# Latent attention: the reciprocal row sums are spread behind the products with the values

## The chip, the cores and the metric

The kernel runs on one core of one Trainium2 chip. Its time is the device time of one execution in microseconds (us), as the median of several runs. Each number in the profile comes from one profiled execution.

## The reference

The reference runs two transformer blocks over 1024 positions of width 1024, in float32. The first has a state-space branch and a latent attention branch; the second has windowed attention and a gated feed-forward part. The change lies in the latent attention: four heads, 192 dimensions of queries and keys, 128 of values, causal:

```
s = einsum('bqhd,bkhd->bhqk', qb, k) * scale
s = where(causal, s, -inf)
pr = softmax(s, axis=-1)
out = einsum('bhqk,bkhd->bqhd', pr, v)
ym = out * silu(gm)                      # the gate, taken from another projection
```

## The kernel before

The attention stage is `block1b` (lines 718 to 869). It loops over four heads (`hd`) and, in each, over four groups of 256 queries (`g`): 16 groups. A group has two blocks of 128 queries. For each block TensorE forms the scores (`sp`, line 811), VectorE adds the mask and takes the maximum (`negmax`), ScalarE takes the exponential into `P` and adds up each row into `ls`, TensorE transposes `P` in pieces of 128x128 (`tp`, line 826), and ScalarE and VectorE split the transposed piece into a high and a low float32r half (`PT`).

The softmax is not divided by its sum before the product with the values. Instead the reciprocal of the sum (line 833) stands as one number for each query, on partitions. The output of the product is transposed (128 value dimensions on partitions, 256 queries along the row), so the reciprocal must lie along the row and be the same on all partitions. TensorE does that: it transposes the column, broadcast to 128x128, into PSUM (`lb`, lines 834 to 836). VectorE multiplies `lb` by 0.5 and by the loaded gate into `gl` (line 839). TensorE multiplies values and transposed exponentials into `po` (lines 840 to 844), three matmuls for each of `2g + 2` key blocks, so 6, 12, 18 or 24 of them. VectorE multiplies `po` by `gl` into `y` (line 846, tile `yo` in the profile), which is stored.

`lb` and `po` are tiles of the PSUM pool `mlaps` with the tag `mm`, which has two buffers. The same two buffers serve every projection tile `ps` of the stage: the queries and keys of the next head (`project`), the values (`values`, evacuated by `vl`), the gate of the state-space branch (`glu`, evacuated by `gst`), and the output products (`out_ys`, evacuated by `xst`). The scores have four buffers of their own, the transposed pieces two.

The order on each engine is not that of the text. A planner (`schedule_with_timeline_sim=True`) goes through the program with modelled durations and picks, for each engine, among the instructions whose inputs and buffers are there by its own clock; text that stands earlier goes first. The engines then work through these fixed orders, and semaphores hold back what comes too early. `self.after(a, b)` (line 140) adds an edge to this plan, without a semaphore: `b` stands behind `a`.

Of the kernel before, what the change touches and what calls it, by code (L numbers as in the profile page):

```python
# [10 lines left out]
F32 = mybir.dt.float32  # L11
F32R = mybir.dt.float32r
I32 = mybir.dt.int32
ALU = mybir.AluOpType
# [37 lines left out]
class Kernel:  # L52
# [665 lines left out]
    def block1b(self):  # L718
        nc, tc, I = self.nc, self.tc, self.I
# [4 lines left out]
        pp = self.open("mlaps", space=PSUM, bufs=2)  # L724
# [26 lines left out]
        def project(hd):  # L751
            qk = [[ma.tile([128, 1024], F32R, name=f"{n}{a}", tag=f"{n}{a}", bufs=2) for a in "hl"] for n in "qk"]

            def evac_q(mt, th, ps):
                hs = slice(th * 512, th * 512 + 512)
                self.split_ps(ps, qk[0][0][:, hs], qk[0][1][:, hs])

            def evac_k(mt, th, ps):
                hs = slice(th * 512, th * 512 + 512)
                self.split_ps(ps, qk[1][0][:, hs], qk[1][1][:, hs], scale)  # L760

            self.dense([[hd]], None, 2, CQ, evac_q, pp, pre={hd: [w[:, 256 * hd:] for w in wq]})
            self.dense([[hd]], None, 1, CK, evac_k, pp, pre={hd: [w[:, 128 * hd:] for w in wkv]})
            return qk + [rotated(hd)]

        def values(pair):
            wh, wl = (w[:, 512 + 256 * pair:] for w in wkv)
            for tk in range(4):
                ps = pp.tile([128, 2, 256], F32, name="ps", tag="mm", bufs=2)
                for j in range(2):  # L770
                    s = slice((2 * tk + j) * 128, (2 * tk + j) * 128 + 128)
                    for n, (a, b) in enumerate(((ck[0], wh), (ck[0], wl), (ck[1], wh))):
                        nc.tensor.matmul(ps[:, j], a[:, s], b[:, :256], start=n == 0, stop=n == 2)
                self.split_ps(ps, V[0][:, 2 * tk:2 * tk + 2], V[1][:, 2 * tk:2 * tk + 2])
# [8 lines left out]
        for hd in range(4):  # L783
            if hd == 2:
                values(1)
            for ch in ((0,), (1,), (2,), (3,))[hd]:
                self.ada_acc(ch, True)
            (qh, ql), (kh, kl), qs_ = qk
            vs = slice((hd % 2) * 128, (hd % 2) * 128 + 128)
            for g in range(4):  # L790
                PT = [m2.tile([128, 2 * g + 2, 256], F32R, name=f"pt{a}", tag=f"pt{a}{g % 2}", bufs=1) for a in "hl"]
                ls = m2.tile([128, 2, 2], F32, name="ls", tag="ls", bufs=3)
                if g < 2:
                    nc.gpsimd.memset(ls[:, :, 1], 0.0)
                for x in PT:
                    nc.gpsimd.memset(x[:, 2 * g + 1, 0:128].bitcast(F32), 0.0)
                for j in range(2):
                    qi = 2 * g + j
                    nk = 128 * (qi + 1)
                    nch, w = (1, max(nk, 256)) if nk <= 512 else (2, nk // 2)  # L800
                    we = min(w, nk)
                    qs = slice(qi * 128, qi * 128 + 128)
                    mx = m2.tile([128, 2], F32, name="mx", tag="mx", bufs=3)
                    P = m2.tile([128, 1024], F32, name="P", tag="P", bufs=2)
                    sps = []
                    for c in range(nch):
                        sp = pp.tile([128, 512], F32, name="sp", tag="S", bufs=4)
                        k = slice(c * w, c * w + w)
                        ops = ((qh, kh), (qh, kl), (ql, kh), (qs_, KS[0]), (qs_, KS[1]))
                        for n, (a, b) in enumerate(ops):  # L810
                            nc.tensor.matmul(sp[:, :w], a[:, qs], b[:, k], start=n == 0, stop=n == 4)
                        self.negmax(sp[:, :we], (ctab[:, 640 - we:] if c == nch - 1 else ctab)[:, :we], mx[:, c:c + 1])
                        sps.append(sp)
                    rq = self.rq[:, qi:qi + 1]
                    if nch == 1:
                        self.tt(mx[:, 0:1], mx[:, 0:1], rq, ALU.mult)
                    else:
                        self.stt(mx[:, 0:1], mx[:, 0:1], mx[:, 1:2], rq, ALU.min, ALU.mult)
                    for c in range(nch):
                        self.act(P[:, c * w:c * w + we], sps[c][:, :we], AF.Exp, bias=mx[:, 0:1],  # L820
                                 scale=self.nrq[:, qi:qi + 1], accum=ls[:, j, c:c + 1])
                    for k0 in range(0, qi + 1, 4):
                        n = min(4, qi + 1 - k0)
                        tp = pp.tile([128, 4, 128], F32, name="tp", tag="T", bufs=2)
                        for k in range(n):
                            nc.tensor.transpose(tp[:, k], P[:, (k0 + k) * 128:(k0 + k + 1) * 128], self.ident)
                        self.split_ps(tp[:, :n], PT[0][:, k0:k0 + n, j * 128:j * 128 + 128],
                                      PT[1][:, k0:k0 + n, j * 128:j * 128 + 128])
                ls2 = m2.tile([128, 2], F32, name="ls2", tag="ls2", bufs=3)
                self.tt(ls2, ls[:, :, 0], ls[:, :, 1], ALU.add)  # L830
                ls = ls2

                nc.vector.reciprocal(ls, ls)
                lb = pp.tile([128, 2, 128], F32, name="lb", tag="mm", bufs=2)
                for j in range(2):
                    nc.tensor.transpose(lb[:, j], ls[:, j:j + 1].to_broadcast([128, 128]), self.ident)
                gl = m2.tile([128, 256], F32, name="gl", tag="gl", bufs=2)
                nc.sync.dma_start(gl, self.g2_d[4 + hd][:, 256 * g:256 * g + 256])
                self.stt(gl, lb.rearrange("p a b -> p (a b)"), 0.5, gl, ALU.mult, ALU.mult)
                po = pp.tile([128, 256], F32, name="po", tag="mm", bufs=2)  # L840
                for k in range(2 * g + 2):
                    for n, (a, b) in enumerate(((V[0], PT[0]), (V[0], PT[1]), (V[1], PT[0]))):
                        nc.tensor.matmul(po, a[:, k, vs], b[:, k, :], start=k == 0 and n == 0,
                                         stop=k == 2 * g + 1 and n == 2)
                y = m2.tile([128, 256], F32, name="yo", tag="yo", bufs=2)
                self.tt(y, po, gl, ALU.mult)
                nc.sync.dma_start(self.ysm_d[4 + hd][:, 256 * g:256 * g + 256], y)
                if g == 1 and hd < 3:
                    qk = project(hd + 1)
                if (hd, g) == (2, 1):  # L850
                    self.wo = {mt: self.load_w(self.wo_src(mt), 1024) for mt in range(4)}
                if (hd, g) == (2, 3):

                    self.load_ys(1, self.cqp, "cq")
                for mt in YSF.get((hd, g), ()):
                    self.out_ys(mt, pp)
                for ch in {(2, 0): (0,), (3, 0): (1,), (3, 2): (2,)}.get((hd, g), ()):
                    self.ada_fin(ch, pp, "T", 2)
            if hd < 2:
                self.glu(hd, pp)  # L860
            if hd == 1:
                self.load_ys(0, ysp, "y0")
# [1291 lines left out]
```

## Time and profile before

| what | value |
|---|---|
| median of three runs | 2269.06 us (2267.28 to 2270.81) |
| the profiled execution | 2265.56 us |
| its span, first to last instruction | 2263.5 us |
| mean granted TensorE clock | 0.972 |
| TensorE matmul busy | 2122.7 us (94%), 10216 instructions |
| VectorE busy | 1502.9 us (66%) |
| ScalarE busy | 969.7 us (43%) |
| GpSimd busy | 1124.1 us (50%) |

In the profile PE is TensorE's matmul, PEld its weight load, DVE is VectorE, ACT ScalarE, POOL GpSimd, SP SyncE. L836 is line 836 of the kernel; lines 83, 86, 102 and 111 are those of helpers that many places call, so one goes by the tile's name there. A wait for several semaphores is put down to the one that came last. Idle time of an engine that is not the bottleneck costs nothing.

### The profile page before, as it was taken

Reading aid. Unit: us, or ns where it says so; the run is one execution under the profiler, and the core shown is the slowest. Engines: PE = TensorE matmul, PEld = TensorE weight load, DVE = VectorE, ACT = ScalarE, POOL = GpSimd, SP = SyncE. Lnnn points to the kernel's source line nnn. Section 1 sums busy time; section 2 is a strip of 40 time slices with the busy share of each in tenths; the row PEclk is TensorE's granted clock in tenths of the full one; section 3 lists DMA queues with packets and bytes.
Section 4 is the critical chain, followed back from the end, with each engine's and each line's share of the span. In section 5 each row is a group of like instructions: output and inputs, shape, how many; then the busy total and the mean of one; then the engine's idle time right before and its main releaser. Section 6 shows DMA issues by size and latency. Waiting matters only on the chain.

```text
span 2263.5 us, 29117 instructions
## 1 busy us (share of the span) xinstructions
PE 2122.7 (94%) x10216; PEld 1766.0 (78%) x10216; DVE 1502.9 (66%) x2511; ACT 969.7 (43%) x1717; POOL 1124.1 (50%) x728
## 2 busy tenths in 40 slices
PE   5998999899999989999999898999899999989998
PEld 4776777777877778888887786888688888877887
DVE  8969976652486345545656862435987777777676
ACT  4222345432245356666444442223544444455223
POOL 4625556665554545654423333523455555535471
PEclk8999999999999999999999899999999999999999
DMA  7433345555654555555345545442122222234332
GB/s 274 137 101 108 92 122 177 177 172 182 199 172 166 175 167 170 171 171 150 121 136 158 166 159 181 169 139 102 47 84 84 84 84 84 84 130 135 98 126 80
DMA packets 186973, 313.25 MB, mean 138 GB/s; under 512 B 43512, under 2 KB 85068, under 8 KB 186828
## 3 DMA queue, kind: packets, MB, share of 16 engines
q1 hardware_dynamic: 186828, 311.40, 43.0%
q8 instruction: 80, 1.31, 0.2%
q14 instruction: 65, 0.53, 0.1%
HBM read 225.65 MB, written 80.96 MB: 135 GB/s over the span
## 4 chain that ended last, share of the span: by engine, by line
PE 41%; DVE 6%; DMA 2%; issue 1%; ACT 1%; POOL 1%; SPq 0%; POOLq 0%; DVEq 0%; ACTq 0%
PE u L1704 17%; PE ps L137 4%; PE ps L135 4%; PE ps L136 4%; PE pd L1885 3%; PE pd L136 2%; PE pd L135 2%; PE pd L137 2%; PE po L1386 1%; DMA ox<-o_d 1%; DVE P L90 1%; PE tp L1378 1%; DVE x L86 1%; DMA as<-a_d 1%; DVE a L86 1%
## 5 line engine op out<-in xcount | busy, mean ns | idle before, releaser
L111 POOL TENSOR_TENSOR wl<-wst,wh 128x1024 fp32r<-128x1024 f32 (+2 forms) x159 | 398.3, 2507 | 488.8 <-ACT wh L102 454.4
L102 ACT ACTIVATE wh<-wst 128x1024 fp32r<-128x1024 f32 (+1 forms) x164 | 168.3, 1028 | 274.2 <-PE ps L136 115.2
L83 POOL TENSOR_TENSOR acc<-acc,wa 128x512 f32<-128x512 f32 x84 | 110.5, 1316 | 16.6 <-ACT wa L102 13.3
L135 PE MATMUL ps<-xh,wh 128*128 128x512 f32 x256 | 103.3, 404 | 4.2 <-DVE kb L83 2.7
L135 PE MATMUL ps<-h1h,wh 128*128 128x512 f32 x256 | 102.5, 400 | 2.8 <-DVE qz L86 2.1
L135 PE MATMUL ps<-h0h,wh 128*128 128x512 f32 x256 | 103.9, 406 | 0.6 <-ACT wh L102 0.6
L137 PE MATMUL ps<-h0h,wl 128*128 128x512 f32 x256 | 102.9, 402 | 0.7 <-POOL wl L111 0.6
L136 PE MATMUL ps<-h0l,wh 128*128 128x512 f32 x256 | 103.1, 403 | 0.0
L136 PE MATMUL ps<-h1l,wh 128*128 128x512 f32 x256 | 102.7, 401 | 0.0
L137 PE MATMUL ps<-xh,wl 128*128 128x512 f32 x256 | 102.0, 399 | 0.0
L136 PE MATMUL ps<-xl,wh 128*128 128x512 f32 x256 | 101.9, 398 | 0.0
L137 PE MATMUL ps<-h1h,wl 128*128 128x512 f32 x256 | 101.9, 398 | 0.0
L83 POOL TENSOR_TENSOR tb<-rt,grid 128x384 f32<-128x384 f32 x48 | 43.1, 906 | 117.0 <-DVE mx L886 88.9
L135 PE MATMUL pd<-Ah,wh 128*128 128x512 f32 (+1 forms) x256 | 93.8, 366 | 5.4 <-ACT s L102 5.4
L136 PE MATMUL pd<-Al,wh 128*128 128x512 f32 (+1 forms) x256 | 93.8, 366 | 0.5 <-DVE Al L111 0.5
L137 PE MATMUL pd<-Ah,wl 128*128 128x512 f32 (+1 forms) x256 | 92.8, 366 | 0.0
L83 DVE TENSOR_TENSOR z<-r,wst 128x512 f32<-128x512 f32 x40 | 71.6, 1790 | 24.5 <-POOL wl L111 24.0
L886 DVE CUSTOM_DVE_ANT_0 sp<-sp,tab 128x256 f32<-128x256 f32 (+1 forms) x128 | 52.7, 425 | 41.8 <-PE sp L163 26.4
L90 POOL TENSOR_SCALAR wa<-wa,sc 128x512 f32<-128x512 f32 x36 | 56.9, 1582 | 47.0 <-DMA wa<-in_w_ada 45.3
L111 POOL TENSOR_TENSOR wl<-z,wh 128x1024 fp32r<-128x1024 f32 (+1 forms) x28 | 63.9, 2282 | 30.8 <-ACT wh L102 27.2
L102 ACT ACTIVATE a<-a 128x1024 f32<-128x1024 f32 x22 | 23.4, 1063 | 108.9 <-DVE a L86 108.8
L83 DVE TENSOR_TENSOR s<-s,pd 128x512 f32<-128x512 f32 x76 | 51.0, 681 | 27.9 <-PE pd L137 14.1
(595 smaller groups left out, 7086.3 us busy)
## 6 DMA issues: line engine op xcount, KB each, us to landing
wa<-in_w_ada SPq DMA_DIRECT2D x96, 256.0 KB, 3.1
wst<-in_w_in SPq DMA_DIRECT2D x47, 512.0 KB, 4.0
wst<-in_w_up SPq DMA_DIRECT2D x24, 512.0 KB, 3.3
a_d<-a SPq DMA_DIRECT2D x22, 512.0 KB, 2.6
wst<-in_w_down SPq DMA_DIRECT2D x22, 512.0 KB, 3.6
as<-a_d SPq DMA_DIRECT2D x22, 512.0 KB, 3.6
r<-in_w_up SPq DMA_DIRECT2D x20, 512.0 KB, 3.2
wst<-in_w_out SPq DMA_DIRECT2D x16, 512.0 KB, 3.3
```

The costliest lines, as they stand in the source:

```text
L83: (eng or self.nc.vector).tensor_tensor(out, a, b, op)
L86: self.nc.vector.scalar_tensor_tensor(out, a, s, b, op0=op0, op1=op1)
L90: (eng or self.nc.vector).tensor_scalar(out, a, s1, None, op0=op0)
L102: self.nc.scalar.activation(out, a, f, **kw)
L111: self.last_lo = e.tensor_tensor(lo, y, hi.bitcast(F32), ALU.subtract)
L135: first = mm(ps, wh, xh, start=start, stop=False)
L136: mm(ps, wh, xl, start=False, stop=False)
L137: mm(ps, wl, xh, start=False, stop=stop)
L886: self.nc.vector.tensor_tensor_reduce(out=s, in0=s, in1=tab, scale=-1.0, scalar=-NEG, op0=ALU.add, op1=ALU.min, accum_out=m)
L1378: nc.tensor.transpose(tp[:, g], P[:, g], self.ident)
L1704: nc.tensor.matmul(ps, x[:, s], y[:, k], start=first and n == 0, stop=k == 3 and n == 2, skip_group_check=True)
L1885: nc.tensor.matmul(ps, w[u][:, 128 * k:128 * k + 128], x[v], start=start and k == i == 0, stop=k == 1 and i == 2, skip_group_check=True)
```

## The change

The transposes into `lb` and the product of `lb` with the gate are moved behind the matmuls into `po`. Both transposes get an edge behind the group's last matmul, so they follow it in TensorE's order. The tile `po` now takes its buffer ahead of `lb`. The load of the gate keeps its place in the text, behind the reciprocal.

```diff
                 nc.vector.reciprocal(ls, ls)
-                lb = pp.tile([128, 2, 128], F32, name="lb", tag="mm", bufs=2)
-                for j in range(2):
-                    nc.tensor.transpose(lb[:, j], ls[:, j:j + 1].to_broadcast([128, 128]), self.ident)
                 gl = m2.tile([128, 256], F32, name="gl", tag="gl", bufs=2)
                 nc.sync.dma_start(gl, self.g2_d[4 + hd][:, 256 * g:256 * g + 256])
-                self.stt(gl, lb.rearrange("p a b -> p (a b)"), 0.5, gl, ALU.mult, ALU.mult)
                 po = pp.tile([128, 256], F32, name="po", tag="mm", bufs=2)
                 for k in range(2 * g + 2):
                     for n, (a, b) in enumerate(((V[0], PT[0]), (V[0], PT[1]), (V[1], PT[0]))):
-                        nc.tensor.matmul(po, a[:, k, vs], b[:, k, :], start=k == 0 and n == 0,
-                                         stop=k == 2 * g + 1 and n == 2)
+                        last = nc.tensor.matmul(po, a[:, k, vs], b[:, k, :], start=k == 0 and n == 0,
+                                                stop=k == 2 * g + 1 and n == 2)
+                lb = pp.tile([128, 2, 128], F32, name="lb", tag="mm", bufs=2)
+                for j in range(2):
+                    t = nc.tensor.transpose(lb[:, j], ls[:, j:j + 1].to_broadcast([128, 128]), self.ident)
+                    self.after(last, t)
+                self.stt(gl, lb.rearrange("p a b -> p (a b)"), 0.5, gl, ALU.mult, ALU.mult)
                 y = m2.tile([128, 256], F32, name="yo", tag="yo", bufs=2)
```

## Rows read from the trace of the kernel before

**Rows 1.** The page, part 1: busy us, share of the span, instructions, by engine.
```profile
PE 2122.7 (94%) x10216; PEld 1766.0 (78%) x10216; DVE 1502.9 (66%) x2511; ACT 969.7 (43%) x1717; POOL 1124.1 (50%) x728
```

**Rows 2.** Busy time by stretch (us, count) of each engine; TensorE's clock, DMA share, GB/s.
```profile
325.00:500.00 175.00, 155.21 (x925) 133.76 (x926) 118.77 (x296) 90.26 (x202) 126.36 (x114) 0.98 0.57 174
...
500.00:540.00 40.00, 39.32 (x169) 31.25 (x168) 10.64 (x19) 5.65 (x8) 16.54 (x12) 1.00 0.49 170
...
660.00:700.00 40.00, 31.46 (x128) 24.47 (x127) 37.04 (x47) 23.83 (x37) 19.91 (x7) 0.87 0.41 141
```

**Rows 3.** Costs by line, 325 to 500 us: count, busy us, mean ns, idle before, releasers.
```profile
L83 DVE TENSOR_TENSOR yo<-po,gl 128x256 f32<-128x256 f32 x16 | 6.7, 421 | 14.7 <-PE po L843 14.6
L86 DVE SCALAR_TENSOR_TENSOR gl<-lb,gl 128x256 f32<-128x256 f32 x16 | 6.6, 415 | 0.6 <-PE lb L836 0.6
L836 PE MATMUL lb<-ident,ls 128*128 128x128 f32 x32 | 6.6, 289 | 5.4 <-DVE kl L86 3.0 <-DVE vl L83 1.3 <-DVE gst L86 0.6
```

**Rows 4.** Waits of TensorE, 325 to 500 us: who for whom, us in total, times, longest.
```profile
PE lb L836 <- DVE kl L86: 3.0, 1, 3.0
PE lb L836 <- DVE vl L83: 1.3, 1, 1.3
...
PE po L843 <- DVE vl L83: 0.9, 1, 0.9
...
PE po L843 <- DVE yo L83: 0.7, 2, 0.4
PE po L843 <- DVE xst L86: 0.7, 1, 0.7
...
PE lb L836 <- DVE yo L83: 0.5, 1, 0.5
PE po L843 <- DVE gst L86: 0.4, 1, 0.4
```

**Rows 5.** TensorE in order, 438 to 444 us: start, us, what, idle before and releaser.
```profile
439.14 0.43 PE L836 MATMUL lb<-ident,ls 128*128 128x128 f32 x2 [1.29 <-DVE vl L83]
440.43 0.39 PE L843 MATMUL po<-pth,vh 128*128 128x256 f32 x1 [0.85 <-DVE vl L83]
...
441.24 0.38 PE L836 MATMUL lb<-ident,ls 128*128 128x128 f32 x2
441.92 0.39 PE L843 MATMUL po<-pth,vh 128*128 128x256 f32 x1 [0.30 <-DVE yo L83]
...
443.43 0.39 PE L135 MATMUL ps<-cq,wh 128*128 128x512 f32 x1
```

**Rows 6.** TensorE in order, 343 to 488 us, around three groups.
```profile
343.99 0.39 PE L135 MATMUL ps<-cq,wh 128*128 128x512 f32 x1
...
470.05 0.39 PE L135 MATMUL ps<-ys,wh 128*128 128x512 f32 x1
...
473.39 0.38 PE L836 MATMUL lb<-ident,ls 128*128 128x128 f32 x2
...
477.93 0.28 PE L843 MATMUL po<-pth,vh 128*128 128x256 f32 x1
...
480.86 0.50 PE L135 MATMUL ps<-ys,wh 128*128 128x512 f32 x1 [0.70 <-DVE yo L83]
...
483.50 0.39 PE L137 MATMUL ps<-ys,wl 128*128 128x512 f32 x1
...
487.44 0.63 PE L836 MATMUL lb<-ident,ls 128*128 128x128 f32 x2
```

**Rows 7.** VectorE in order, 345 to 487 us, around the same groups.
```profile
345.00 0.41 DVE L83 TENSOR_TENSOR yo<-po,gl 128x256 f32<-128x256 f32 x1
...
480.40 0.40 DVE L83 TENSOR_TENSOR yo<-po,gl 128x256 f32<-128x256 f32 x1
...
486.56 0.69 DVE L86 SCALAR_TENSOR_TENSOR xst<-xst,ps 128x512 f32<-128x512 f32 x1
```

**Rows 8.** SyncE's queue in order, 440 to 500 us: the load that xst reads.
```profile
483.53 0.32 SPq L876 DMA_DIRECT2D xst<-xn_d  x1
```

## The prediction

> **What bounds the kernel now.** I read the busy times first: TensorE works for 94% of the span and no other engine comes near it [rows 1]. The reader is to see there that a microsecond counts only if TensorE stands still in it. Then the busy times by stretch [rows 2]: the attention stage runs from about 325 to 500 us, and TensorE is busy for 155.21 of its 175 us, so 19.8 us stand idle; VectorE and GpSimd have 119 and 126 us of work in it, so neither is the bound of the stage as a whole. Behind it, from 500 to 540 us, TensorE is busy for 39.32 of 40 us: what the stage gains or loses on TensorE is passed on to the end nearly whole, as nothing idle stands there to take it up.
>
> Third, the costs by line [rows 3]: the 32 transposes that spread the reciprocals (lb, two in each of 16 groups of head and query block) take 6.6 us of TensorE in all, the 16 products that read them on VectorE (gl) 6.6 us, the 16 that read the products with the values (yo) 6.7 us. Fourth, TensorE's waits: it stands still four times ahead of lb, for 3.0 + 1.3 + 0.6 + 0.5 = 5.4 us [rows 3, 4], and five times ahead of po, for 0.9 + 0.7 + 0.7 + 0.4 = 2.7 us [rows 4]. None of the nine is for the reciprocal or for the exponentials. The names (kl, vl, gst, yo, xst) are those of VectorE instructions that read another tile of the tag "mm": lb, po and every ps of the projections share two PSUM buffers, and these are waits for one of the two. So 8.1 of the 19.8 idle us are a matter of who holds the buffers, and that is what the change rearranges.
>
> **The change, part by part.** Nothing is added or removed: the same 32 transposes, 16 gl, 16 yo and the same 16 loads of gl and 16 stores of y. The load of gl is now issued ahead of the transposes in the text, but it had no input from them before either, and gl as a buffer is untouched: nothing. The extra edge is between two instructions of one engine and needs no semaphore: nothing. That leaves order and buffers.
>
> Before, lb takes a buffer, gives it back after gl, and po can then run in the same one: a group gets by with a single buffer. The trace shows it at work [rows 6, 7]: from 470.05 us one buffer holds the output of the first out_ys until xst reads it at 486.56 us, and in that time lb (473.39), po (477.93) and the next ps (480.86) follow one another through the other. After the change po holds its buffer while lb asks for a second one, and po's is not free before gl and yo have both run. A group now needs two at once, at its end.
>
> *Tail of a group.* Before, yo starts as po ends. After, the two transposes (0.38 us for a pair, first start to last end [rows 5]), gl (415 ns) and yo (421 ns) stand in a row [rows 3]: po's buffer comes free about 0.38 + 0.42 = 0.8 us later. Whoever wants a buffer right behind po now waits for gl, about 0.8 us from the start of lb, where before lb's buffer had long been free.
>
> *Back-to-back groups, 438 to 444 us* [rows 5]. Before: lb waits 1.29 us, po another 0.85, the second po 0.30; ps follows at 443.43. After: po starts at 439.14 in lb's place, its six matmuls last the 441.24 - 440.43 = 0.81 us that they last now, and lb can follow only when vl has freed the second buffer, at the 440.43 that po waited for. Then gl is through at 440.43 + 0.8 = 441.2, the second po runs there instead of at 441.92 (0.7 us gained), ends 443.43 - 441.92 = 1.5 us later at 442.7, its lb follows, and ps gets gl's buffer at 442.7 + 0.8 = 443.5. That is 0.1 us later than now; if transposes of the next block are put into the gap, 0.3 us earlier. I take 0.2 us gained. The pair at 384 to 391 us has the same form with waits of 0.6, 0.5 and 0.4 us [rows 3, 4]: again 0.2 us gained. The 0.7 us ahead of the last po (xst) goes, but out_ys behind it then waits 0.8 us for gl in place of nothing, with the lb pair (0.2 us of it on the array) moved in front: 0.1 us gained. The 3.0 us wait for kl stays: the scores that stand behind lb in the queue read kl as well.
>
> *First head, second group* [rows 6, 7]. The projection's ps at 343.99 us runs in lb's buffer while yo ends only at 345.4. After the change both buffers are held until gl and yo have passed VectorE's queue, about 345.4 us, so 1.4 us later. Scores that need no such buffer stand ready; if they move ahead it costs 0, if not 1.4. I take 0, and keep 1.4 for the range.
>
> *Last head, second group* [rows 6 to 8]. This is the dear one. Po starts at 477.93 and, with 12 matmuls as the po of [rows 5] that lasts 1.5 us, ends at about 479.4 us; lb needs a second buffer while out_ys holds it until xst at 486.56, whose input is loaded only by the issue at 483.53. In the present order the second out_ys uses that time (12 matmuls from 480.86). It can't start any more, as po's buffer waits for lb. Its 12 matmuls start 0.24 us apart ((483.50 - 480.86) / 11), about 2.9 us in all; they are then done later, and TensorE has little else to do meanwhile: 2.9 us lost. Bounds: 0 if the planner sets the first out_ys behind lb; the whole stretch from 480.86 to xst's end, 487.25, if nothing at all can be put there: 6.4.
>
> Sum: -0.2 - 0.2 - 0.1 + 0 + 2.9 = +2.4 us. On the profiled execution's 2265.56 us (2.06 of it outside its span of 2263.5) that is 2268.0; it lies 3.5 us under the median of the three runs, and 2269.06 + 2.4 gives 2271.5.
>
> The rows show waits of one kind, again and again, for one of two buffers [rows 4]. The Trainium skill ("Perfetto Trace Analysis", section "Optimization Strategy") says that the same gap repeating on the engine that should be saturated can mean too little SBUF or PSUM for the next tile to be allocated. It speaks against a change that leaves the two buffers and has both held at once; by it the time would be that of rival B. By the rows alone it is the sum above.
>
> **The rivals.** A is the sum: small gains, one loss, 2271.5.
>
> B, slower: the second buffer is missing at the end of a group, as at 480 us, and VectorE's queue makes it worse: gl and yo stand in it ahead of the splits and maxima of the next block. Place: groups beside glu and out_ys, where a ps holds a buffer. Price: 6.4 us there, and 0.6 us (0.8 less a moved pair of 0.2) at each of five places where a ps stands right behind po, as at 443.43 us [rows 5] (the others lie near 391, 412, 491 and 498 us): +9.4, 2278.5. It decides as soon as the second buffer comes free later than po ends in more than one group. For it: the one-buffer working of [rows 6]. Against: po starts earlier without lb before it.
>
> C, faster: po takes the buffer that lb took, the second one is always free by the time po is through, and the waits ahead of lb and po go without new ones: all 8.1 us at most, less the 3.0 for kl, which has its own reason: -5.1, 2264.0. For it: po runs for 0.8 us or more [rows 5], longer than six of the nine waits. Against: the back-to-back case, where the next po or ps inherits the wait.
>
> D: the planner lays out the whole program by its own clock, and a shifted stage leads it to another order further on. At 660 to 700 us TensorE is idle for 8.5 of 40 us beside a VectorE of 37.04 [rows 2]; a few us more or less in such a place is 2269.06 ± 6 (an estimate: some two thirds of that idle time, either way). That the change does not do what it says would need lb to be late already; in every group shown it stands ahead of po.
>
> **How the numbers follow.** Chances: A 0.42, B 0.24, C 0.22, D 0.12. About 0.2%, 4.5 us, is what a measurement of this kernel can tell from no change. A lies within it (0.36) unless its loss is over 4.5 (0.06 slower). B is slower in 0.18, within in 0.06; C faster in 0.19, within in 0.03; D half and half. Faster 0.25, same 0.45, slower 0.30. For the range I go down by all 8.1 us of waits and 3 of D (2258), and up by B's 9.4 and the 1.4 of the first head (2280). Within A alone the time runs from 2269 (loss 0, gains kept) to 2277 (the loss 6.4 and 1.4, less the gains).
>
> **What would show it.** Right: in the waits from 325 to 500 us "lb" no longer stands with kl or gst, "po" with kl or vl takes its place, and a new wait of ps or po for gl appears, 0.3 to 0.8 us each; TensorE's busy time in the stage stays near 155 us. The last head shows a gap near 480 us or out_ys shifted behind yo. Wrong, to the fast side: the idle 19.8 us shrink by over 4.5 with no wait for gl. Wrong, to the slow side: lb itself waits, behind po, for gst or xst, more than once. D would show as a stage of the same length and a difference behind 540 us.

## The result, and the profile after

The changed kernel takes 2282.93 us (median of 4 runs, 2280.79 to 2285.08); the kernel before, run beside it, takes 2268.17 (4 runs, 2263.12 to 2270.81). The ratio is 1.0068 [1.0056, 1.008]: 14.8 us slower. The forecast was 2271.5 with a range up to 2280. It was too low, and so was rival B, which had the right mechanism (2278.5).

The profiled execution took 2282.65 us (span 2280.6). First the page's part 1, for TensorE, and the busy times by stretch, with the columns of [rows 2]; 325 to 517 us is now the length of the attention stage.

```profile
PE 2132.5 (94%) x10216; PEld 1774.8 (78%) x10216; DVE 1506.5 (66%) x2511; ACT 970.5 (43%) x1717; POOL 1124.6 (49%) x728
```

```profile
325.00:500.00 175.00, 150.17 (x850) 129.48 (x850) 117.19 (x289) 89.03 (x200) 119.60 (x110) 0.93 0.52 160
500.00:540.00 40.00, 38.45 (x174) 31.27 (x174) 12.74 (x25) 3.16 (x5) 12.39 (x10) 0.91 0.45 155
660.00:700.00 40.00, 34.73 (x161) 28.52 (x159) 36.46 (x42) 21.30 (x32) 24.09 (x9) 0.93 0.58 195
```

```profile
325.00:517.00 192.00, 165.62 (x924) 142.26 (x925) 122.05 (x298) 90.96 (x203) 126.26 (x115) 0.92 0.51 159
```

The reader is to see two losses. For the same work (924 matmul records here, 925 in [rows 2]) TensorE needs 192 us in place of 175: it stands idle for 26.4 us in place of 19.8, and it is busy for 165.6 us in place of 155.2. No matmul was added. What grew is the time of each one: the granted clock of the stage fell from 0.98 to 0.92.

To compare all kernels I measure one stretch that always holds the same work: from the first scores matmul of the stage to the first matmul of the feed-forward part (`ps` from `wh` and `h0l`). "Idle" is the time in it in which no matmul runs, "half clock" the time for which the trace shows the granted clock at the lower of its two levels, 1.2 in place of 2.4 GHz, and "busy in it" the part of that time in which a matmul runs. "Rest" is the time from its end to the end of the span. "lb late" adds up, over the groups, the time from the end of po's last matmul to the start of lb, where lb comes later. "Tail" adds up, over the 16 groups, the time from po's end to the end of yo, which frees po's buffer. Each row is one profile.

| kernel | stretch | idle | half clock | busy in it | rest | lb late | tail |
|---|---|---|---|---|---|---|---|
| before | 363.7 | 26.4 | 17.1 | 14.4 | 1574.2 | 0 | 11.5 |
| after | 379.6 | 32.1 | 41.0 | 35.4 | 1574.1 | 19.4 (7 groups) | 50.1 |
| E1 after, one bank | 368.1 | 29.3 | 27.3 | 21.2 | 1578.9 | 0 | 24.5 |
| E6 before, one bank | 368.3 | 29.4 | 23.9 | 18.3 | 1571.2 | 0 | 14.9 |
| E13 after, lb in T | 387.7 | 41.3 | 34.1 | 28.9 | 1571.0 | 0 | 32.8 |
| E14 before, lb in T | 371.6 | 30.1 | 27.3 | 23.5 | 1573.4 | 0 | 15.3 |
| E16 after, own xst | 373.9 | 33.5 | 25.1 | 20.0 | 1571.6 | 6.8 (6 groups) | 40.0 |
| E17 before, own xst | 364.0 | 28.5 | 17.1 | 13.3 | 1570.8 | 0 | 12.4 |
| E18 before, both edits | 368.6 | 28.3 | 27.3 | 22.2 | 1574.0 | 0 | 13.0 |
| E19 after, both edits | 365.2 | 28.1 | 20.5 | 16.8 | 1567.0 | 0 | 28.6 |

Before to after the stretch grows by 15.8 us (unrounded) and the rest by nothing: the whole loss lies in the attention stage. Of the 15.8 us 5.7 are idle time and 10.1 busy time (337.3 to 347.4). The clock accounts for the busy part: 21.0 us more of it ran at half clock, where matmuls of one form follow each other about half as fast (128x512: 0.43 us apart at a clock of 0.50, below, against 0.24 in [rows 6]), which by an estimate, half of the 21.0, makes some 10 us. Without half of "busy in it" every kernel of the table, before and after included, is busy for 328 to 332 us. The same matmuls stand 1.4 us later at 320 us, about 7 at 430, 11 at 470 and 18 from 490 on (median shift of equal matmuls), so the loss builds up over the whole stage, most of it in the second half.

The lines that answer to [rows 3], for 325 to 517 us:

```profile
L86 DVE SCALAR_TENSOR_TENSOR gl<-lb,gl 128x256 f32<-128x256 f32 x16 | 6.7, 419 | 13.8 <-PE lb L843 11.8 <-DMA uu_d<-xst 1.9
L83 DVE TENSOR_TENSOR yo<-po,gl 128x256 f32<-128x256 f32 x16 | 6.7, 419 | 0.2
L843 PE MATMUL lb<-ident,ls 128*128 128x128 f32 x32 | 6.5, 285 | 3.1 <-DVE vl L83 2.2 <-DVE gst L86 0.9
```

The three cost what they cost before. Only the waiting has moved: VectorE now stands idle ahead of gl, for lb, where it stood idle ahead of yo, for po. TensorE's waits, which answer to [rows 4] (the groups with kl and yo are gone):

```profile
PE ps L135 <- DVE ql L83: 3.7, 3, 2.2
PE ps L135 <- DVE gl L86: 2.9, 5, 0.9
...
PE lb L843 <- DVE vl L83: 2.2, 2, 1.2
PE aps L998 <- DVE ptl L83: 1.9, 1, 1.9
...
PE po L839 <- DVE gst L86: 1.1, 1, 1.1
...
PE lb L843 <- DVE gst L86: 0.9, 1, 0.9
PE po L839 <- DVE vl L83: 0.9, 1, 0.9
...
PE po L839 <- DVE gl L86: 0.3, 1, 0.3
```

The new wait of ps and po for gl stands there six times, 0.3 to 0.9 us each. Read alone, these waits would make the loss about 3 us. The largest group is that of ps for ql, which reads another ps of the same two buffers; before it had one wait of 0.3 us. What was not ready to run while lb waited the view does not show. That is seen in order. TensorE in the last head, second group, which answers to the last rows of [rows 6]:

```profile
486.54 0.28 PE L839 MATMUL po<-pth,vh 128*128 128x256 f32 x1
...
488.75 0.29 PE L839 MATMUL po<-pth,vl 128*128 128x256 f32 x1
...
491.43 0.41 PE L826 MATMUL tp<-ident,P 128*128 128x128 f32 x2 [0.46 <-DVE ptl L83]
493.73 1.84 PE L998 MATMUL aps<-ones_d,acc 128*128 128x1 f32 x8 [1.89 <-DVE ptl L83]
495.43 1.73 PE L826 MATMUL tp<-ident,P 128*128 128x128 f32 x7
498.01 1.97 PE L826 MATMUL tp<-ident,P 128*128 128x128 f32 x8 [0.84 <-DVE ptl L83]
499.77 0.63 PE L843 MATMUL lb<-ident,ls 128*128 128x128 f32 x2
500.92 0.80 PE L135 MATMUL ps<-ys,wh 128*128 128x512 f32 x1 [0.52 <-DVE gl L86]
501.51 0.63 PE L136 MATMUL ps<-ys,wh 128*128 128x512 f32 x1
501.94 0.63 PE L137 MATMUL ps<-ys,wl 128*128 128x512 f32 x1
```

Lb starts 10.7 us behind po's end (499.77 - 489.04). In between TensorE has the scores that were left, transposes, a small product (aps) and 3.2 us of gaps ahead of the rows shown; then the 12 matmuls of the second out_ys, which before ran from 480.86 on [rows 6], come at 0.43 us apart and 0.63 us each, where the same form took 0.39 us [rows 6]. Lb had to wait for the first out_ys to give up its buffer: SyncE issued xst's load at 494.37 us, before at 483.53 [rows 8], and VectorE read the buffer at 498.33 (486.56 in [rows 7]). SyncE's queue, then VectorE, of the changed kernel:

```profile
494.37 0.33 SPq L877 DMA_DIRECT2D xst<-xn_d  x1
```

```profile
498.33 0.68 DVE L86 SCALAR_TENSOR_TENSOR xst<-xst,ps 128x512 f32<-128x512 f32 x1
...
500.44 0.42 DVE L86 SCALAR_TENSOR_TENSOR gl<-lb,gl 128x256 f32<-128x256 f32 x1
...
501.38 0.41 DVE L83 TENSOR_TENSOR yo<-po,gl 128x256 f32<-128x256 f32 x1
```

And the clock there, by windows of 10 us:

```profile
485.00:495.00 10.00, 7.66 (x45) 6.52 (x44) 7.76 (x18) 4.92 (x13) 9.40 (x9) 0.92 0.55 133
495.00:505.00 10.00, 8.64 (x30) 6.98 (x31) 4.62 (x11) 3.97 (x9) 6.17 (x5) 0.50 0.57 176
```

From 495 to 505 us TensorE counts as busy for 8.64 of 10 us, at a clock of 0.50: the idle time has turned into slow matmuls, which no view of waits counts.

### The profile page after: what moved, and what is told of

It reads as the page before. It is cut to its first block, busy times and chain, and to the rows that moved or that the text cites. A ratio compares the mean times of both kernels' runs of the same rounds, so it can differ in the third digit from the quotient of the medians.

```text
span 2280.6 us, 29115 instructions
## 1 busy us (share of the span) xinstructions
PE 2132.5 (94%) x10216; PEld 1774.8 (78%) x10216; DVE 1506.5 (66%) x2511; ACT 970.5 (43%) x1717; POOL 1124.6 (49%) x728
## 4 chain that ended last, share of the span: by engine, by line
PE 42%; DVE 6%; DMA 2%; issue 1%; ACT 1%; POOL 0%; SPq 0%; POOLq 0%; DVEq 0%; ACTq 0%
PE u L1705 17%; PE ps L137 5%; PE ps L135 5%; PE ps L136 5%; PE pd L1886 3%; PE pd L136 2%; PE pd L135 2%; PE pd L137 2%; PE po L1387 1%; PE tp L1379 1%; DVE x L86 1%; DVE a L86 1%; DVE Al L111 0%; DVE P L90 0%; DVE kl L83 0%
## 5 line engine op out<-in xcount | busy, mean ns | idle before, releaser
L102 ACT ACTIVATE P<-sp,st 128x256 f32<-128x256 f32 (+1 forms) x128 | 59.0, 464 | 25.1 <-DVE st L887 23.8
```

Of the source, the lines that this page charges most:

```text
L102: self.nc.scalar.activation(out, a, f, **kw)
```

## The experiments

The kernel before was run beside each group; "before" is its median there (2265.9 to 2270.9 us, so compare within a group).

**Is it two buffers at once, or the later transposes?** E2 keeps the transposes where they were but reads lb only at the end, so that lb and po hold both buffers; E3 is the change without the added edge.

```diff
 # E2, against before: gl is not multiplied by lb any more
-                self.stt(gl, lb.rearrange("p a b -> p (a b)"), 0.5, gl, ALU.mult, ALU.mult)
 ...
                 self.tt(y, po, gl, ALU.mult)
+                self.stt(y, lb.rearrange("p a b -> p (a b)"), 0.5, y, ALU.mult, ALU.mult)
 # E3, against after
-                    self.after(last, t)
```

Expected, E2:

> The kernel before, transposes ahead of po as there, but lb is read only at the end: y = po * gate, then y = y * lb * 0.5 (two VectorE operations as before, in other order), so lb keeps its buffer beside po until then. Theory of the two buffers: slower by 6 to 15 us, 2274 to 2283. Theory of the order: within 3 us of 2268.

Expected, E3:

> The changed kernel without the edge: the transposes stand behind po in the text, but the planner may set them elsewhere. Theory of the two buffers: po still takes its buffer first, lb the second, so as the changed kernel, 2279 to 2286. If the edge itself costs the time: within 3 us of 2268.

Measured: E2 2286.72 against 2270.59, ratio 1.0065 [1.005, 1.008]; E3 2285.14, 1.0054 [1.0037, 1.007]. Holding both is enough for a loss of this size, with early transposes (E2's stretch: 381.9 us, 41.0 at half clock). But E2 holds both for longer, 58.3 us in sum over the groups against 18.2 after the change, so the size alone proves little. The edge plays no part; the text's order alone does it (E3's lb stands 18.3 us late in sum).

**One bank for both.** Po and lb have 256 columns each; together they fill one buffer of 512. E1 does this with the change's order, E6 with before's.

```diff
-                po = pp.tile([128, 256], F32, name="po", tag="mm", bufs=2)
-                lb = pp.tile([128, 2, 128], F32, name="lb", tag="mm", bufs=2)
+                pl = pp.tile([128, 512], F32, name="pl", tag="mm", bufs=2)
+                po, lb = pl[:, 0:256], pl[:, 256:512].rearrange("p (a b) -> p a b", a=2)
```

Expected, E1:

> The changed kernel, but po and lb are two halves of one tile of 512 float32 (one buffer of the tag mm), the transposes still behind po by the edge. Theory of the two buffers (a group must hold two of the two mm buffers at its end): a group now holds one, so the loss of 14.8 us is gone, 2265 to 2273 us, and no wait of ps for gl stays in the stage. Theory of the order (transposes behind po give a worse order or a longer tail whatever the buffers): 2278 us or more.

Expected, E6:

> The kernel before with po and lb as two halves of one tile, transposes ahead of po as there; a group holds one buffer, but from lb to yo. Theory of the two buffers: the place of the transposes decides nothing when one buffer holds both, so within 4 us of the run with one bank and the transposes behind po (2276). Theory of the order: 5 us or more below that run.

Measured: E1 2275.95 against 2270.59, 1.0021 [1.0011, 1.003]; E6 2267.91 against 2270.89, 0.9988 [0.9976, 1.0]. Two thirds of the loss are gone. The 8 us between the two spoke for a cost of the order itself, but the table says where they are not: the stretch is the same (368.1 and 368.3), lb follows po directly in all 16 groups of E1, and the profiles differ in the rest, 1578.9 against 1571.2 (7.3 of these 7.7 us are idle time of TensorE).

**Which heads?** E4 makes the change in the last head alone, E5 in the first three.

```diff
+                late = hd == 3        # E4; hd < 3 in E5
```

Expected, E4:

> The change for the last of the four heads alone, the three others as before. The traces put about 8 of 16 us lost in the stage behind 489 us, in the last head, where lb waits 10.7 us for out_ys's buffer: 2274 to 2278. If the three first heads carry the loss: 2268 to 2271. If the last head alone makes it: 2280 or more.

Expected, E5:

> The change for the first three heads alone, the last as before. If the two parts of the change add up, what the last head alone left of the 14.8 us comes from here: 2274 to 2280. If the first three heads carry nothing of their own: 2267 to 2271.

Measured: E4 2278.33 against 2270.59 (+7.7), 1.0026 [1.0011, 1.0042]; E5 2280.61 against 2270.89 (+9.7), 1.0046 [1.0032, 1.006]. The two add up to 17.4, near the 14.8 of the change. In their profiles, though, the stretch grows by 10.8 us (E4) and 17.0 (E5), 27.8 together against 15.8 for the whole change, so that the parts simply add up is not shown. The last head alone is not the loss: the first three heads, which the forecast had at -0.4, cost as much.

**A third buffer.** E7 is the change and E8 the kernel before, both with three buffers for mm and three in place of four for the scores.

```diff
-        pp = self.open("mlaps", space=PSUM, bufs=2)
+        pp = self.open("mlaps", space=PSUM, bufs=3)
-                        sp = pp.tile([128, 512], F32, name="sp", tag="S", bufs=4)
+                        sp = pp.tile([128, 512], F32, name="sp", tag="S", bufs=3)
 # and bufs=3 for po, lb and the two ps
```

Expected, E7:

> The changed kernel with three buffers of the tag mm, one taken from the scores (tag S, 4 to 3). Theory of the two buffers: a group's second buffer is no longer the last one, so against the next kernel (the kernel before with the same three) nothing over 4 us is left; in absolute terms 2264 to 2276, as the scores lose a buffer. Theory of the order: 10 us or more over the next kernel.

Expected, E8:

> The kernel before with three buffers of the tag mm and three of the scores: the control of the run ahead of it. Both theories: 2262 to 2274, as it waits less for mm and more for the scores.

Measured: E7 2275.38 against 2270.69, 1.0026 [1.0008, 1.0045]; E8 2274.43, 1.001 [0.9997, 1.0024]. With a third buffer the change costs 1.0 us (2275.38 - 2274.43), but E7's runs spread from 2267.96 to 2285.96 and the two ranges of the ratio overlap, so some us either way are not excluded. E8 itself, with a buffer less for the scores, stands 3.7 us above the kernel before. (E7's profiled execution lay 10 us above its median, so its rows are not used.)

**Out_ys out of the way.** E9 and E10 move all four out_ys behind the last group, with and without the change.

```diff
-        YSF = {(3, 0): (0,), (3, 1): (1,), (3, 2): (2,), (3, 3): (3,)}
+        YSF = {(3, 3): (0, 1, 2, 3)}
```

Expected, E9:

> The changed kernel with the four out_ys of the last head all behind its last group in the text, so that none holds a buffer while lb asks for one; the gate branch (glu) still does so in the first two heads. Theory of the two buffers: lb's wait of 10.7 us in the last head is gone and about 8 of the 16 us lost in the stage stay, against the next kernel (same move, kernel before) +3 to +9 us. Theory of the order: +13 or more against it.

Expected, E10:

> The kernel before with the four out_ys moved as in the run ahead of it: its control. Both theories: 2268 to 2278, since out_ys no longer fills the waits of the last head.

Measured: E9 2288.31 against 2270.69, 1.0076 [1.0049, 1.0103]; E10 2272.88, 1.0008 [0.9991, 1.0025]. The difference stays at 15.4 us, so the idea that out_ys's held buffer makes up the last head's loss fell in this form. Lb is no longer late there, but out_ys was also the work that fills the last head: from 325 to 520 us E9 runs for 37.5 us at half clock, E10 for 10.2 (after: 30.7, before: 6.8).

**More work for the last head.** E11 and E12 put matmuls of 128x512 between the transposes of the last head (36 of them in the profile, not the 42 of the expectation; some 8 us of work by the 0.23 us between two such matmuls); their results are overwritten by the transposes.

```diff
                         for k in range(n):
+                        # ahead of it
+                        if hd == 3 and n == 4:
+                            for _ in range(6):
+                                nc.tensor.matmul(tp.rearrange("p a b -> p (a b)"), KS[0][:, 0:128], KS[0][:, 0:512],
+                                                 start=True, stop=True)
```

Expected, E11:

> The changed kernel with extra work on TensorE: ahead of each full transposed piece of the last head (tile tp of four, seven of them) six matmuls of 128x512 into the same tile, overwritten by the transposes. They add about 42 x 0.22 = 9 us of work that can run while TensorE waits. Theory of the clock (idle spells let the granted clock fall to 1.2 GHz, and that makes more of the loss than the idle time): the half-clock time between 465 and 515 us falls from 20 us to under 10, and the kernel is not slower than the changed kernel by more than 3 us, perhaps faster. Theory of the waits alone: slower than it by 4 to 9 us, as the next kernel is over the kernel before.

Expected, E12:

> The kernel before with the same extra matmuls: the control. Its half-clock time in the last head is 3.4 us, so the clock has little to give back: 2271 to 2279 by both theories.

Measured: E11 2285.28 against 2270.89, 1.0073 [1.005, 1.0096]; E12 2273.11, 1.0015 [1.0002, 1.0027]. The windows from 465 to 515 us, first of after, then of E11, then of E12:

```profile
465.00:515.00 50.00, 42.44 (x216) 37.12 (x216) 28.66 (x69) 18.50 (x42) 32.75 (x28) 0.80 0.47 144
```

```profile
465.00:515.00 50.00, 43.58 (x240) 38.11 (x239) 27.59 (x69) 18.70 (x42) 35.05 (x29) 0.90 0.46 137
```

```profile
465.00:515.00 50.00, 45.19 (x251) 38.64 (x250) 26.94 (x64) 15.49 (x34) 29.33 (x23) 0.97 0.48 148
```

With the fill the clock there is 0.90 in place of 0.80, but E11 is no faster than the changed kernel (14.4 us over its kernel before): the difference to the control is 12.2 us, against 14.8. As a test of the clock's share it is inconclusive; lb still stood 13.1 us behind po.

**Lb in another pair of buffers.** E13 and E14 take lb out of mm and put it into the two buffers of the transposed pieces.

```diff
-                lb = pp.tile([128, 2, 128], F32, name="lb", tag="mm", bufs=2)
+                lb = pp.tile([128, 2, 128], F32, name="lb", tag="T", bufs=2)
```

Expected, E13:

> The changed order, but lb takes a buffer of the transposed pieces (tag T) in place of one of the two mm buffers. Theory of the buffers: po and lb no longer ask for two mm buffers at a time, so most of the loss of 14.8 us goes; the time lies within 4 us of the kernel with the old order and lb in a T buffer (the run beside it), and lb has no wait of several us behind po in the last head. Theory of the order: the transposes behind the products are late for gl, yo and the store whichever buffer they use; 8 us or more above the run beside it.

Expected, E14:

> Control: the kernel before with lb in a T buffer. lb then competes with the transposed pieces. Both theories: within 6 us of the kernel before, in either direction; it is the base for the run with the changed order and the same buffers.

Measured: E13 2287.86 against 2265.9, 1.0096 [1.0083, 1.0109]; E14 2274.11, 1.0035 [1.0023, 1.0048]. The theory of the buffers expected most of the loss to go; it stayed, 13.8 us. E13's waits of TensorE from 325 to 525 us:

```profile
PE tp L826 <- DVE gl L86: 3.6, 4, 2.1
PE po L839 <- DVE kl L86: 3.6, 2, 3.2
...
PE po L839 <- DVE xst L86: 3.0, 1, 3.0
```

Lb does follow po directly now, but it holds one of the two buffers of the transposed pieces until gl, and those wait for gl (3.6 us); po keeps its buffer for 97.1 us in sum over the groups (66.4 in E14, 47.8 before). So taking away the request for a second mm buffer is not enough while lb takes a scarce buffer of another kind and po still waits for lb, gl and yo. That the tail by itself, and not the T buffers, costs here is not shown.

**An early load of xst.** E16 and E17 give xst two buffers of its own, so its load need not stand behind others for a staging buffer.

```diff
-        x = self.wp.tile([128, 2, 512], F32, name="xst", tag="wst", bufs=2)[:, 0]
+        x = self.m2x.tile([128, 512], F32, name="xst", tag="xst", bufs=2)     # self.m2x = m2
```

Expected, E16:

> The change, with the tile xst that out_ys loads given two buffers of its own, so that its load need not stand behind those of yx for a staging buffer. Theory of the held buffer: the 10.7 us for which lb waits behind po in the last head are a wait for xst's load; with the load early they shrink below 3 us, and the loss against the run beside it falls from 14.8 to 6 to 9 us (that of the first three heads stays). Theory that the last head loses by its lack of other work and the lower clock: the loss stays at 12 us or more.

Expected, E17:

> Control: the kernel before with the same two buffers for xst. Both theories: 0 to 4 us faster than before, as out_ys gives its buffer back sooner there too; it is the base for the run with the change.

Measured: E16 2275.21 against 2265.9, 1.0037 [1.002, 1.0054]; E17 2263.46, 0.9994 [0.9982, 1.0005]. TensorE in E16, the same group of the last head:

```profile
486.43 0.29 PE L840 MATMUL po<-pth,vl 128*128 128x256 f32 x1
486.67 0.38 PE L844 MATMUL lb<-ident,ls 128*128 128x128 f32 x2
```

The 10.7 us are gone, as the theory of the held buffer said, but the loss against E17 only falls from 14.8 to 11.8 us, short of the 6 to 9 expected (E16's eight runs spread over 12 us; against the kernel before it is 9.3). Lb is late in six other groups, 6.8 us in sum, and the tail is still 40.0.

**Both edits.** E18 and E19 have one bank for po and lb and own buffers for xst, in before's order and in the change's.

Expected, E18:

> Before's order, with po and lb as two halves of one bank, and xst in two buffers of its own: the two edits that each came out a little under the kernel before (2267.91 against 2270.89, and 2263.46 against 2265.9). If both shorten the time for which an mm buffer is held, they add to 4 to 6 us under the kernel before; if they were noise, it is within 3 us of it.

Expected, E19:

> The change's order with the same two edits. Theory of the held buffer (po's buffer comes free later, and lb asks for a second): with one bank for both and the load of xst early nothing of that is left in the attention stage, so the stretch from the first scores to the first feed-forward matmul is within 3 us of that in the run beside it, and the time within 8 us (the one-bank pair differed by 8 us, most of it in the part from 1600 us on). Theory of the order: that stretch is 8 us or more longer.

Measured: E18 2270.18 against 2270.79, 0.9999 [0.9988, 1.001]; E19 2260.82, 0.9959 [0.9945, 0.9973]. E19 from 325 to 500 us, with the columns of [rows 2]:

```profile
325.00:500.00 175.00, 155.25 (x922) 134.79 (x921) 123.80 (x298) 89.90 (x201) 124.36 (x115) 0.97 0.56 174
```

This is the stage of before again, 155.25 us busy at a clock of 0.97, with the change's order in it. The order costs nothing there (365.2 us against 368.6 in E18 and 363.7 before), so the theory of the order is false for these buffers. E19 is the fastest version of all, 10 us under the kernel before; but by the profiles this gain does not lie in the stage: its stretch is 1.5 us longer than before's, its rest 7.2 us shorter. Against E18 it has 3.4 us in the stretch and 7.0 in the rest, where TensorE, VectorE, ScalarE and GpSimd run the same tiles in the same order in both from 600 us on. E18's rest has 3.7 us more idle time of TensorE and 73.2 in place of 60.0 us at half clock; why, in the same order, is open, and these are single profiles. Open is also the 7.7 us in the rest between E1 and E6, whose plans do differ behind 600 us.

## Why the prediction was wrong

*What bounds the kernel:* right as to the engine, and what the stage lost on TensorE reached the end whole (rest 1574.2 and 1574.1). Its premise that a microsecond counts only if TensorE stands still did not hold: 10.1 of the 15.8 us were lost while it worked.

*Nothing for the edge and the load of gl:* right for the edge (E3). The load was not tried alone.

*The tail of a group, 0.8 us later:* right as its smallest size, 0.7. Where nothing intervenes the tail is 1.14 us against 0.46. But it was taken for all groups, and in 11 of 16 it is longer, up to 12.8 us; the sum went from 11.5 to 50.1 us. Po's buffer is one of two, so this is the resource that went missing.

*Back-to-back groups, 0.2 us gained each:* wrong. Po took over lb's wait, as forecast, but lb behind it waits again. The pair behind 438 us stands as before behind the glu and value matmuls, and looks like this, against [rows 5]:

```profile
446.06 0.38 PE L839 MATMUL po<-pth,vh 128*128 128x256 f32 x1 [0.88 <-DVE vl L83]
...
448.27 0.43 PE L843 MATMUL lb<-ident,ls 128*128 128x128 f32 x2 [1.23 <-DVE vl L83]
...
450.38 0.41 PE L839 MATMUL po<-ptl,vh 128*128 128x256 f32 x1
```

Both wait for vl. With 0.17 us for the transposes in between, the idle time of the pair is 2.28 us, against 2.44 before, so by idle time alone the 0.2 us are nearly there. But the 12 matmuls of the second po take 2.7 us in place of 1.7, most of them at 0.41 us, where the form takes 0.28 in [rows 6]. The other pair, taken to be of the same form, is not: the planner put ten glu matmuls and six transposes between po and lb.

```profile
389.22 0.39 PE L839 MATMUL po<-pth,vh 128*128 128x256 f32 x1 [1.09 <-DVE gst L86]
...
394.02 0.43 PE L843 MATMUL lb<-ident,ls 128*128 128x128 f32 x2 [0.88 <-DVE gst L86]
```

Lb starts 3.8 us behind po's end there, and po's buffer comes free 6.1 us behind it. The 3.0 us wait for kl, which was to stay, is gone; nearby a ps waits 2.2 us for ql. The first three heads were priced at -0.4 and cost +9.7 by themselves (E5).

*First head, second group, 0 to 1.4 us:* within its bounds; a ps waits for gl there as forecast, 0.9 us.

*Last head, second group, +2.9 us (bounds 0 and 6.4):* the right mechanism, mis-sized. The change in the last head alone cost 7.7 us (E4). Two things were left out. The wait was measured on the old position of xst's load, and that load moved with everything else, by 10.8 us (494.37 - 483.53). And the displaced 12 matmuls were priced at 0.24 us; they ran 0.43 us apart, so 5.1 us in place of 2.9.

*"TensorE's busy time in the stage stays near 155 us":* wrong, and this is the step that failed for the whole stage. The sum counted idle time alone, +2.4 us of it, and put slower matmuls at nothing. Idle time grew by 5.7 us, and busy time by 10.1 us, as 21.0 us more of it ran at half clock. Every kernel of the table whose stretch is over 1 us longer than before's has more idle time and more time at half clock. But the sum of idle time does not set the time at half clock: E10 has 32.6 us idle in the stretch, as much as the changed kernel, and 20.5 at half clock. What brings the clock down is not shown (E11 was meant to and doesn't decide).

*Rival B* named the place and the sign: a second buffer missing at the end of several groups. What was to decide for it, a second buffer that comes free later than po ends in more than one group, stands in seven groups. At 2278.5 it is 4.4 us short, and its sum too holds idle time alone. The rule of the Trainium skill that stood beside it ("Perfetto Trace Analysis", section "Optimization Strategy": the same gap again and again can mean too little PSUM) agrees with what E19 shows: with one buffer for both tiles and an early load the loss in the stage is gone (stretch 365.2 us, 379.6 after the change). *Rival C* is false: waits went and others came. *Rival D* is false for this change: TensorE's order behind the stage does differ in a few places, but the rest takes the same time. By its own terms the upper end of A is 2276.4 (2269.06 + 6.4 + 1.4 - 0.5), not 2277.

So the cause: after the change a group keeps po's buffer until lb, gl and yo have passed, and asks for a second one of the same pair meanwhile. Shown, for the stage, by E1 with E6 and E18 with E19 (one bank for both: the order costs nothing in the stretch) and by E16 (with the early load lb's 10.7 us are gone). In line with it are E2 (holding both costs as much with early transposes) and E7 with E8 (1.0 us left with a third buffer, within a spread of some us). Not settled: what brings the lower clock, and how much of E13's loss is the tail and how much the T buffers. Each edit also gives another plan: among the kernels in before's order the stretch runs from 363.7 us to 374.5 (E8), so some us of any one pair can be the plan's.

## What to carry to other kernels

When a tile that lives briefly is moved behind one that lives long, and both come from the same small set of buffers, write down who holds which buffer from when to when, at every group and with the loads that free them, before adding up durations; here the tail went from 11.5 to 50.1 us without a single instruction being added. Put tiles that are needed together into one buffer: with that and an early load the stretch of the changed order fell from 379.6 to 365.2 us. (The 10 us by which that kernel beats the one before lie behind the stage, and their cause is open.) And do not price a lost buffer by idle time alone where work is thin: here 5.7 us of it came with 10.1 us of slower matmuls.

## What the runs showed that I had not expected

- The same 1709 matmuls took 337.3 us of busy time before and 347.4 after. A busy share near 94% on both pages hides this; the granted clock by windows (0.98 and 0.92) and the duration of one form (0.39 and 0.63 us for 128x512) show it.
- One load of SyncE's queue, issued at 494.37 in place of 483.53 us, held a PSUM buffer, and through it lb, po and the next product.
- Kernels with the same order of tiles on the four computing engines from 600 us on (E18 and E19) differ by 7.0 us in the rest of their profiles, and by 9.4 us in their medians. A difference of a few us between two versions must first be located before a mechanism is named for it.
